# Constants of a two-layer hybrid decoder made in pieces, and attention's two masks turned into one mask and a difference of values

## The chip, the core and the metric

The kernel runs on one core of a Trainium2 chip. The core's engines are TensorE (PE, matmuls; PEld is its weight load), VectorE (DVE), ScalarE (ACT), GpSimd (POOL) and SyncE (SP, which only issues DMAs here); each takes its instructions in order, and they wait for one another by semaphores. The metric is the device time of one execution in microseconds, median of several runs.

## What is computed

Two decoder layers on 1024 tokens of width 1024, then a final norm. Per layer, from the reference (cut):

```python
h = rms_norm(x, norm_w[layer])
proj = h @ w_in[layer]
(q, k, v, z_attn, q_h, f_h, i_h, g_h, gate_attn, gate_hgrn) = jnp.split(proj, split_points, axis=-1)
q, k = partial_rope(q, positions), partial_rope(k, positions)      # 8 heads, 2 KV heads of 64
a = sliding_window_attention(q, k, v, attn_sinks[layer]) * silu(z_attn)   # window 128
logf = log(lb + (1 - lb) * sigmoid(f_h)); kin = (1 - lb) * sigmoid(-f_h); qin = silu(q_h)
o = hgrn2_recurrence(qin, kin, i_h, logf)                          # 4 heads of 128
b = rms_norm_per_head(o) * hgrn_norm_w[layer] * silu(g_h)
merged = sigmoid(gate_attn) * (a @ w_up_attn) + sigmoid(gate_hgrn) * (b @ w_up_hgrn)
x = x + merged @ w_out[layer]
```

`lb` comes from a softmax over the layers, the rotary angles from `positions`, and a query sees its own position and the 127 before it. In blocks of 128 a query of block b therefore sees of block b its own keys up to itself, and of block b-1 the keys behind its own index: each of the 128 index pairs belongs to exactly one of the two.

## The kernel before

Matmuls work on fp32 numbers split in a high and a low part (`whi`, `wlo` of the weights, L128 and L129; three matmuls for each product). A layer runs through these stages: norm and transposes; 13 *pairs* of 128-column chunks of the input projection; rotary, and the projection for `z`; attention, in whose gaps stand the value projection `pi` of the recurrence (L762) and the forget and query projections of its head 0 (L769); the recurrence of the four heads (`core`, L835), with other projections between; the up and out projections.

**A pair** (`pair_rest`, L271) computes two chunks for 1024 tokens by five products of half size, 12 matmuls of 128x512 each. Its weights are two loaded chunks `wr`; DVE adds their halves to `ws` (L277 to L281), ACT casts sums and halves to the high parts (`whi`, L128; `wh`, L285), DVE makes the low parts (`wlo`, L129; `wl`, L286). The products go to two PSUM banks, `pb` and `pc`, and DVE adds them to three outputs `pq` (L303), which ACT puts through sigmoid or silu and sends off (`gate_out`, L473 and L474). Buffers: two for each kind of full weight chunk (`wp`), one for `wh` and `wl`, four for outputs (`hp`, tag `po`).

**Constants.** In the first layer, `constants()` (L356 to L429) is called after pair 1 and `tables()` (L431 to L450) after pair 5. The first loads masks and small inputs, makes `lb` and `oml`, the angles `ang` (eight multiplications, L407), their reduction to one period (`nrn`, L410 to L421), and two Sin on ACT (L426, L427), each change of function family costing an ACT_TABLE_LOAD. The second makes four tables `tab` on POOL and DVE, which PE transposes (`tt`, L447) and ACT sends to memory, where `rotary` reads them in pair 12.

**Attention** goes in steps u: `turn(u-4)` transposes the probabilities of a block (`tp`, L721), `value(u)` projects, then come `values(u-4)`, `scores(u-1)`, `softmax(u-2)`. The probabilities of the window stand in one 128x128 matrix a head: each entry is that of the past block or of the own one. DVE multiplies the transposes by the mask of the past and by the mask of the own block (`side`, two masks) into two halves of `pT` (L724), and `values` (L728) multiplies the first with `vn` of block b-1, the second with `vn` of block b into one bank `av`; ACT copies that to `avo` (L738).

The order of instructions on each engine is made by a scheduler when the program is built, from the order of the code, buffers and its own costs; only operations under `tc.keep_in_program_order` stay as written. PE's order thus follows from the order on other engines, and the reverse.

Of the kernel before, what the change touches and what calls it, by code (L numbers as in the profile page):

```python
# [17 lines left out]
P = 128  # L18
# [20 lines left out]
def trunk_kernel(ctx, tc, x, positions, norm_w, w_in, attn_sinks, hgrn_norm_w, w_up_attn,  # L39
# [315 lines left out]

    def constants():  # L356
# [3 lines left out]
        side = cp.tile([P, 2, P], F32, name="side")  # L360
# [18 lines left out]
        nc.sync.dma_start(lbl, lb_logits.rearrange("l (h p) -> p l h", p=P))  # L379

# [20 lines left out]


# [3 lines left out]
        for b in range(NB):  # L406
            V.tensor_scalar(out=ang[:, b], in0=freq, scalar1=posf[:, b:b + 1], scalar2=None, op0=ALU.mult)  # L407
        nrn = cp.tile([P, NB, HALF], F32, name="nrn")
# [5 lines left out]
        for bits in (2, 8, 8, 24):  # L414
            if bits == 24:
                c = float(np.float32(rest))
            else:
                e = math.floor(math.log2(rest))
                q = 2.0 ** (e - (7 if bits == 8 else 7))
                c = math.floor(rest / q) * q  # L420
            V.scalar_tensor_tensor(out=ang, in0=nrn, scalar=-c, in1=ang, op0=ALU.mult, op1=ALU.add)  # L421
            rest -= c
        V.tensor_scalar(out=ang, in0=ang, scalar1=3.1415925, scalar2=-3.1415925, op0=ALU.min, op1=ALU.max)
# [5 lines left out]
        return ones, side, upper, never, mdiag, mlev, sink, hnw, lb, oml, sins, nrn  # L429

    def tables(sins, nrn):  # L431
        for i in range(2):
            for g in range(2):
                b = slice(4 * g, 4 * g + 4)
# [21 lines left out]
    def first_chunk(L, m, slots):  # L456

        nm = f"p{L}_{m}"
        return (split_slot if slots else split_w)(load_chunk(w_in[L], pairs[m][0][0], nm), nm, [P, KT, P])


    for L in range(DEPTH):
# [135 lines left out]
        for m in range(NPAIR):  # L598
            (c0, r0), (c1, r1) = pairs[m]
            o = pair_rest(wi, (c0, c1), parts, hT, f"{L}_{m}", p1s[m])  # L600
            if m > 9:
                tr[r1] = slot([P, T], f"tr_{L}_{r1}")
            for key, r, t0 in (("22", r1, 512), ("12", r0, 512), ("21", r1, 0)):
                if m < 10:
                    gate_out(o[key], o[key], r, t0)
                else:
                    S.activation(tr[r][:, t0:t0 + 512], o[key], AF.Copy, scale=qkv[r][1])
            if m == 12:
                cosT, sinT = rotary()
            if L == 0 and m == 1:  # L610
                ones, side, upper, never, mdiag, mlev, sink, hnw, lb, oml, *angles = constants()
            elif L == 0 and m == 5:
                tables(*angles)
# [35 lines left out]

        w = [chunk(wi, OZ + j * P, f"z{L}_{j}") for j in range(2)]  # L650
# [16 lines left out]
        z(3, w[3], [H0, H1])  # L667

# [45 lines left out]
        def turn(b):  # L714
            pr, _ = probs[b]
            probs[b] = []
            for g in range(2):

                tp = bank([P, 2, 2, P], f"tp_{L}_{b}_{g}")
                for j in range(4):  # L720
                    PE.transpose(tp[:, j % 2, j // 2], pr[:, 4 * g + j], ident)  # L721
                pT = slot([P, 2, 4, P], f"pT_{L}_{b}_{g}")
                for pt in ([0, 1] if b else [1]):
                    V.tensor_tensor(out=pT[:, pt], in0=tp.rearrange("p r i q -> p (r i) q"),  # L724
                                    in1=side[:, pt].unsqueeze(1).broadcast_to([P, 4, P]), op=ALU.mult)
                probs[b].append(pT)

        def values(b):  # L728
            av = bank([P, 4, P], f"av_{L}_{b}")
            for g, pT in enumerate(probs.pop(b)):  # L730
                for pt in ([0, 1] if b else [1]):
                    for r in range(2):
                        PE.matmul(av[r * HD:(r + 1) * HD, 2 * g:2 * g + 2].rearrange("p h q -> p (h q)"),  # L733
                                  lhsT=vn[0][:, b if pt else b - 1, g * HD:(g + 1) * HD],
# [438 lines left out]
def _constants():  # L1173
    p = np.arange(P)
    past = p[:, None] > p[None, :]
    side = np.stack([past, ~past], axis=1).astype(np.float32)
# [36 lines left out]
```

## Time and profile before

| | |
|---|---|
| three runs, us | 1463.02, 1467.82, 1465.97; median 1465.97 |
| the profiled execution, us | 1462.61 |
| its span, us | 1460.8 |
| busy in the span | PE 97%, PEld 78%, DVE 64%, ACT 46%, POOL 5% |
| time PE waited longest for, by line | `lv_n` on DVE's `gs`: 5.9 us in 6 waits |

A span is the time from the first to the last instruction of one profiled execution. In the rows below, "a <- b" after an operation reads output and input; what stands in square brackets is how long its engine was idle before it, and which instruction on which engine released it. `x4` is the number of such instructions in a row. Matmuls are pipelined: the time of one in a row is the distance between two starts, not the length that the row gives. Names leave buffer numbers out, so `pb`, `wlo_s` and the like recur in every pair.

### The profile page before, as it was taken

Reading aid. Unit: us, or ns where it says so; the run is one execution under the profiler, and the core shown is the slowest. Engines: PE = TensorE matmul, PEld = TensorE weight load, DVE = VectorE, ACT = ScalarE, POOL = GpSimd, SP = SyncE. Lnnn points to the kernel's source line nnn. Section 1 sums busy time; section 2 is a strip of 40 time slices with the busy share of each in tenths; the row PEclk is TensorE's granted clock in tenths of the full one; section 3 lists DMA queues with packets and bytes.
Section 4 is the critical chain, followed back from the end, with each engine's and each line's share of the span. In section 5 each row is a group of like instructions: output and inputs, shape, how many; then the busy total and the mean of one; then the engine's idle time right before and its main releaser. Section 6 shows DMA issues by size and latency. Waiting matters only on the chain.

```text
span 1460.8 us, 21289 instructions
## 1 busy us (share of the span) xinstructions
PE 1420.7 (97%) x8252; PEld 1146.4 (78%) x8252; DVE 933.4 (64%) x1586; ACT 676.4 (46%) x1354; POOL 66.7 (5%) x77
## 2 busy tenths in 40 slices
PE   8999999999999999999999999999999999999998
PEld 7877778878777778778888878887787677787876
DVE  6856656646656887673656466565467588867643
ACT  8754333246664554432556332333567545433321
POOL 1100000310000000000000000003000000000000
PEclk9999999999999999999999999999999999999999
DMA  8433443463236643336454333436522465444431
GB/s 271 158 109 116 141 145 113 155 166 129 81 114 204 222 175 131 120 113 231 158 199 151 102 130 125 149 94 200 164 73 94 138 203 195 140 148 152 159 144 58
DMA packets 194277, 214.41 MB, mean 147 GB/s; under 512 B 12480, under 2 KB 142016, under 8 KB 194176
## 3 DMA queue, kind: packets, MB, share of 16 engines
q1 hardware_dynamic: 161152, 161.66, 34.8%
q10 hardware_dynamic: 31488, 46.15, 8.6%
q0 software_dynamic: 1536, 5.24, 0.9%
q8 instruction: 65, 1.06, 0.3%
q14 instruction: 36, 0.29, 0.1%
HBM read 145.65 MB, written 59.77 MB: 141 GB/s over the span
## 4 chain that ended last, share of the span: by engine, by line
PE 75%; DVE 9%; DMA 7%; ACT 6%; issue 2%; ACTq 0%; SPq 0%; DVEq 0%; POOL 0%
PE pb L291 4%; PE pb L292 4%; PE pb L293 4%; PE pg L263 3%; PE pg L265 3%; PE pg L264 3%; PE pc L291 3%; DMA wr<-in_w_in_dram 2%; PE pc L292 2%; PE pc L293 2%; PE pj_qh L139 2%; PE av L733 2%; PE pj_qh L140 2%; PE pj_qh L141 2%; PE pi L140 2%
## 5 line engine op out<-in xcount | busy, mean ns | idle before, releaser
L128 ACT CAST whi_s<-ws 128x1024 fp32r<-128x1024 f32 x26 | 27.4, 1053 | 129.2 <-DVE ws L278 125.0
L724 DVE TENSOR_TENSOR pT<-tp,side 128x512 f32<-128x512 f32 x60 | 39.2, 681 | 23.5 <-PE tp L721 23.5
L139 PE MATMUL pu_ua<-wh_a,wlo_ua 128*128 128x512 f32 x128 | 51.7, 404 | 0.0
L141 PE MATMUL pu_ua<-wh_a,whi_ua 128*128 128x512 f32 x128 | 50.7, 396 | 0.0
L1160 PE MATMUL po<-wlo_o,mg 128*128 128x512 f32 x128 | 49.9, 390 | 0.8 <-DVE wlo_o L129 0.8
L140 PE MATMUL pu_ua<-wl_a,whi_ua 128*128 128x512 f32 x128 | 50.3, 393 | 0.0
L709 ACT ACTIVATE pr<-pr,mx 128x128 f32<-128x128 f32 x128 | 49.9, 395 | 0.8 <-ACT it L759 0.8
L473 ACT ACTIVATE pq<-pq 128x512 f32<-128x512 f32 x60 | 37.8, 631 | 26.6 <-DVE pq L303 25.2
L1159 PE MATMUL po<-whi_o,mg 128*128 128x512 f32 x128 | 50.0, 391 | 0.1
L263 PE MATMUL pg<-hh,wlo_p 128*128 128x512 f32 (+1 forms) x128 | 47.0, 372 | 3.1 <-POOL wlo_p L129 1.7
L1161 PE MATMUL po<-whi_o,mg 128*128 128x512 f32 x128 | 49.6, 389 | 0.0
L694 DVE COPY_PREDICATED pr<-upper,sc 128x256 f32<-128x256 int32 x56 | 23.2, 443 | 40.4 <-ACT pr L693 40.4
L1082 ACT CAST mg<-u 128x512 fp32r<-128x512 f32 x32 | 19.6, 621 | 61.2 <-DVE u L1080 61.1
L264 PE MATMUL pg<-hl,whi_p 128*128 128x512 f32 (+1 forms) x128 | 46.1, 363 | 0.0
L265 PE MATMUL pg<-hh,whi_p 128*128 128x512 f32 (+1 forms) x128 | 46.0, 363 | 0.0
L277 DVE TENSOR_TENSOR ws<-wr 128x512 f32<-128x512 f32 x26 | 17.9, 690 | 42.2 <-DMA wr<-in_w_in_dram 42.2
L303 DVE TENSOR_TENSOR pq<-pb,p 128x512 f32<-128x512 f32 x40 | 27.6, 690 | 26.6 <-PE pb L293 26.6
L129 DVE TENSOR_TENSOR wlo_t<-ws,whi_t 128x1024 fp32r<-128x1024 f32 x26 | 31.8, 1225 | 18.0 <-ACT whi_t L128 17.9
L263 PE MATMUL pg<-hh,wl_p 128*128 128x512 f32 (+1 forms) x112 | 41.3, 369 | 1.7 <-DVE wl_p L337 1.1
L291 PE MATMUL pb<-th,wlo_s 128*128 128x512 f32 x104 | 40.9, 393 | 2.0 <-DVE wlo_s L129 2.0
L291 PE MATMUL pc<-hh,wlo_t 128*128 128x512 f32 x104 | 41.6, 400 | 0.7 <-DVE pq L303 0.6
L291 PE MATMUL pb<-th,wl 128*128 128x512 f32 x104 | 41.1, 395 | 0.8 <-DVE pq L303 0.7
(394 smaller groups left out, 4452.7 us busy)
## 6 DMA issues: line engine op xcount, KB each, us to landing
wr<-in_w_in_dram SPq DMA_DIRECT2D x64, 512.0 KB
gd<-pq ACTq DMA_DIRECT2D x76, 256.0 KB
wr_p<-in_w_in_dram SPq DMA_DIRECT2D x26, 512.0 KB
fq<-fq ACTq DMA_DIRECT2D x48, 256.0 KB
x<-in_x_dram SPq DMA_DIRECT2D x16, 512.0 KB
ga<-gd SPq DMA_DIRECT2D x16, 512.0 KB
u<-gd SPq DMA_DIRECT2D x16, 512.0 KB
wr_o<-in_w_out_dram SPq DMA_DIRECT2D x16, 512.0 KB
```

The source lines that it names most:

```text
L139: PE.matmul(acc, lhsT=ll, rhs=rh, start=i == 0, stop=False)
L140: PE.matmul(acc, lhsT=lh, rhs=rl, start=False, stop=False)
L141: PE.matmul(acc, lhsT=lh, rhs=rh, start=False, stop=i == n - 1)
L263: PE.matmul(acc, lhsT=wl[:, k], rhs=h[:, t], start=k == 0, stop=False, skip_group_check=q > 0)
L264: PE.matmul(acc, lhsT=wh[:, k], rhs=l[:, t], start=False, stop=False, skip_group_check=q > 0)
L265: PE.matmul(acc, lhsT=wh[:, k], rhs=h[:, t], start=False, stop=k % 4 == 3, skip_group_check=q > 0)
L291: PE.matmul(acc, lhsT=wl[:, k], rhs=h, start=start and k == 0, stop=False, skip_group_check=not start)
L292: PE.matmul(acc, lhsT=wh[:, k], rhs=l, start=False, stop=False, skip_group_check=not start)
L293: PE.matmul(acc, lhsT=wh[:, k], rhs=h, start=False, stop=k == 3, skip_group_check=not start)
L709: S.activation(pr[:, h], pr[:, h], AF.Exp, bias=mx[:, h:h + 1], accum_out=sm[:, h:h + 1])
L1159: PE.matmul(accs[j], lhsT=ll, rhs=wh[:, i], start=k + i == 0, stop=False)
L1160: PE.matmul(accs[j], lhsT=lh, rhs=wl[:, i], start=False, stop=False)
```

## The change

**The constants.** `constants()` becomes a generator with eight yields, and `next(consts, None)` runs its next piece after each pair: after pair 0 the loads and masks, after pair 1 `lb` and `oml`, after pair 2 the positions and `ang`, after pair 3 the reduction, after pair 4 the limits, both Sin and a square, after pairs 5 to 8 one table each. What is computed stays the same; names are handed on by a dictionary `made`.

**Attention.** `side` is one mask, that of the own block. A new tile `vd` holds, for blocks 1 to 7, the values of a block minus those of the block before. `turn` copies the transposes whole into the first half of `pT` on ACT and multiplies them by the one mask into the second half on DVE. `values` multiplies the whole with `vn` of block b-1 and the masked part with `vd`. The number of matmuls is the same.

```diff
--- before.py
+++ after.py
@@ constants @@
     def constants():
...
-        side = cp.tile([P, 2, P], F32, name="side")
+        side = cp.tile([P, P], F32, name="side")
...
+        made.update(ones=ones, side=side, upper=upper, never=never, mdiag=mdiag, mlev=mlev, sink=sink, hnw=hnw)
+        yield
...
         V.tensor_scalar(out=oml, in0=lb, scalar1=-1.0, scalar2=1.0, op0=ALU.mult, op1=ALU.add)
+        made.update(lb=lb, oml=oml)
+        yield
...
             V.tensor_scalar(out=ang[:, b], in0=freq, scalar1=posf[:, b:b + 1], scalar2=None, op0=ALU.mult)
+        yield
...
             V.scalar_tensor_tensor(out=ang, in0=nrn, scalar=-c, in1=ang, op0=ALU.mult, op1=ALU.add)
             rest -= c
+        yield
         V.tensor_scalar(out=ang, in0=ang, scalar1=3.1415925, scalar2=-3.1415925, op0=ALU.min, op1=ALU.max)
...
         S.activation(sins, ang, AF.Sin)
         S.activation(nrn, ang, AF.Sin, scale=0.5)
         V.tensor_tensor(out=nrn, in0=nrn, in1=nrn, op=ALU.mult)
-        return ones, side, upper, never, mdiag, mlev, sink, hnw, lb, oml, sins, nrn
-    def tables(sins, nrn):
         for i in range(2):
             for g in range(2):
+                yield
                 b = slice(4 * g, 4 * g + 4)
                 t = hp.tile([P, 4, P], F32, tag="po", name=f"tab_{i}_{g}")
...
@@ the loop over pairs @@
-            if L == 0 and m == 1:
-                ones, side, upper, never, mdiag, mlev, sink, hnw, lb, oml, *angles = constants()
-            elif L == 0 and m == 5:
-                tables(*angles)
+            next(consts, None)
...
@@ behind the z projection @@
+        vd = slot([P, NB - 1, P], f"vd_{L}")
+        V.tensor_tensor(out=vd, in0=vn[0][:, 1:], in1=vn[0][:, :NB - 1], op=ALU.subtract)
...
@@ turn @@
                 pT = slot([P, 2, 4, P], f"pT_{L}_{b}_{g}")
-                for pt in ([0, 1] if b else [1]):
-                    V.tensor_tensor(out=pT[:, pt], in0=tp.rearrange("p r i q -> p (r i) q"),
-                                    in1=side[:, pt].unsqueeze(1).broadcast_to([P, 4, P]), op=ALU.mult)
+                whole = tp.rearrange("p r i q -> p (r i) q")
+                if b:
+                    S.copy(pT[:, 0], whole)
+                V.tensor_tensor(out=pT[:, 1], in0=whole, in1=side.unsqueeze(1).broadcast_to([P, 4, P]), op=ALU.mult)
                 probs[b].append(pT)
...
@@ values @@
-                                  lhsT=vn[0][:, b if pt else b - 1, g * HD:(g + 1) * HD],
+                                  lhsT=(vd if b and pt else vn[0])[:, b - 1 if b else 0, g * HD:(g + 1) * HD],
...
@@ the mask on the host @@
-    past = p[:, None] > p[None, :]
-    side = np.stack([past, ~past], axis=1).astype(np.float32)
+    side = (p[:, None] <= p[None, :]).astype(np.float32)
```

Where the change moves instructions, three places. The first is pair 3 of the first layer, on two engines, DVE first; `ws_3`, `wlo_3` and `wl_3` are the weights of pair 3, `pq_2` and `pq_3` outputs. Before:

```order
L277 TENSOR_TENSOR ws_3_0_1410<-wr_3_1_1408 128x512
L407 TENSOR_SCALAR ang<-freq,posf 128x8 x8
L303 TENSOR_TENSOR pq_2_22_1331<-pc_2_1334,p_0_2_351 128x512
L410 TENSOR_SCALAR nrn<-ang 128x64
L278 TENSOR_TENSOR ws_3_0_1410<-ws_3_0_1410,wr_3_0_1406 128x512
L411 TENSOR_SCALAR nrn<-nrn 128x64
L280 TENSOR_TENSOR ws_3_1_1411<-wr_3_0_1406,wr_3_1_1408 128x512
```

After:

```order
L303 TENSOR_TENSOR pq_2_21_1308<-pb_2_1309,p_0_2_351 128x512
L412 CAST posf<-posi 128x8
L415 TENSOR_SCALAR ang<-freq,posf 128x8 x8
L129 TENSOR_TENSOR wlo_3_t<-ws_3_1_1398,whi_3_t 128x1024
L286 TENSOR_TENSOR wl_3_1412<-wr_3_1_1395,wh_3_1411 128x512
L303 TENSOR_TENSOR pq_3_12_1415<-pb_3_1418,p_0_2_351 128x512
L419 TENSOR_SCALAR nrn<-ang 128x64
```

`ang` and the reduction no longer stand between the sums `ws_3`; `ang` stands ahead of `wlo_3_t` and `wl_3`, the reduction behind them.

The same place on ACT; `wh_3` is the cast on which `wl_3` waits. Before:

```order
L128 CAST whi_3_t<-ws_3_1_1411 128x1024
L474 DMA gd_138<-pq_2_22_1331 128x512
L426 ACT_TABLE_LOAD
L426 ACTIVATE sins<-ang 128x64
L427 ACTIVATE nrn<-ang 128x64
L473 ACT_TABLE_LOAD
L473 ACTIVATE pq_2_12_1330<-pq_2_12_1330 128x512
L473 ACTIVATE pq_2_21_1332<-pq_2_21_1332 128x512
L474 DMA gd_138<-pq_2_12_1330 128x512
L474 DMA gd_138<-pq_2_21_1332 128x512
L285 CAST wh_3_1424<-wr_3_1_1408 128x512
```

After:

```order
L128 CAST whi_3_t<-ws_3_1_1398 128x1024
L483 ACTIVATE pq_2_21_1308<-pq_2_21_1308 128x512
L285 CAST wh_3_1411<-wr_3_1_1395 128x512
L484 DMA gd_138<-pq_2_21_1308 128x512
L436 ACT_TABLE_LOAD
L436 ACTIVATE sins<-ang 128x64
L437 ACTIVATE nrn<-ang 128x64
L483 ACT_TABLE_LOAD
L483 ACTIVATE pq_3_22_1416<-pq_3_22_1416 128x512
L128 CAST whi_4_s<-ws_4_0_1503 128x1024
```

Sin and its two table loads went from ahead of `wh_3` to behind it, ahead of pair 3's first activation and of `whi_4_s`.

The second place is PE in attention: `av_2` are the value products of block 2, `sc_5` the scores of block 5, `pi_7` a value projection. Before:

```order
L140 MATMUL pi_7_3414<-wlo_i_0_2819,hhi_0_2452 128x512
L733 MATMUL av_2_3337<-pT_2_0_3298,vn_2548 64x256 x2
L685 MATMUL sc_5_0_0_3351<-ks_0_0_2491,qs_1_0_2507 128x256
L685 MATMUL sc_5_0_1_3352<-ks_0_1_2492,qs_1_1_2508 128x256
L733 MATMUL av_2_3337<-pT_2_0_3298,vn_2548 64x256 x2
L689 MATMUL sc_5_0_0_3351<-ks_0_1_2492,qs_1_0_2507 128x256
L733 MATMUL av_2_3337<-pT_2_1_3306,vn_2548 64x256 x2
L689 MATMUL sc_5_0_1_3352<-ks_0_0_2491,qs_1_1_2508 128x256
L685 MATMUL sc_5_0_0_3351<-ks_0_0_2491,qs_2_0_2593 128x256
L733 MATMUL av_2_3337<-pT_2_1_3306,vn_2548 64x256 x2
```

After:

```order
L141 MATMUL pi_6_3311<-wh_i_6_2838,hh_1_3_146 128x512
L746 MATMUL av_2_3339<-pT_2_0_3300,vn_2548 64x256 x2
L746 MATMUL av_2_3339<-pT_2_0_3300,vd_2816 64x256 x2
L746 MATMUL av_2_3339<-pT_2_1_3308,vn_2548 64x256 x2
L746 MATMUL av_2_3339<-pT_2_1_3308,vd_2816 64x256 x2
L697 MATMUL sc_5_0_0_3353<-ks_0_0_2491,qs_1_0_2507 128x256
```

The four pieces between the scores became one block ahead of them.

The third place is ACT at the end of attention, where `fq_0_2_512` is the second half of head 0's query, which the recurrence loads first. Before:

```order
L626 ACT_TABLE_LOAD
L626 ACTIVATE fq_0_2_0_3737<-pj_qh_0_0_0_3712 128x512
L738 COPY avo_6_3749<-av_6_3740 128x512
L629 DMA fq_0_2_2462<-fq_0_2_0_3737 128x512
L739 DMA ad_2474<-avo_6_3749 512x1x128
L626 ACTIVATE fq_0_2_512_3793<-pj_qh_0_1_0_3768 128x512
```

After:

```order
L633 ACTIVATE fq_0_2_0_3739<-pj_qh_0_0_0_3714 128x512
L737 COPY pT_7_0_3759<-tp_7_0_3754 128x512
L636 DMA fq_0_2_2462<-fq_0_2_0_3739 128x512
L751 COPY avo_6_3751<-av_6_3742 128x512
L737 COPY pT_7_1_3767<-tp_7_1_3762 128x512
L752 DMA ad_2474<-avo_6_3751 512x1x128
L633 ACTIVATE fq_0_2_512_3795<-pj_qh_0_1_0_3770 128x512
```

Two copies of `pT_7` went ahead of that activation. On PE the transposes `tp_7` (before: near the end of the query's second half) and `av_6` (before: ahead of it) now stand behind the query, in the second forget projection. Elsewhere on PE, in both layers: `av_7` stands in three pieces instead of four, `av_6` in two instead of one; in the first layer the four sets of `tt` stand one each in pairs 6 to 9, after six matmuls, and `tv_0` is moved from pair 6 to the `z` stage. DMAs are issued in the same order as before.

## Rows read from the trace of the kernel before

**Rows 1.** Page: busy us (share of the span) and instructions by engine.

```profile
PE 1420.7 (97%) x8252; PEld 1146.4 (78%) x8252; DVE 933.4 (64%) x1586; ACT 676.4 (46%) x1354; POOL 66.7 (5%) x77
```

**Rows 2.** Windows: start:end, length, busy PE, PEld, DVE, ACT, POOL, clock, DMA.

```profile
124.50:138.97 14.47, 13.89 (x62) 11.18 (x60) 11.61 (x41) 7.12 (x9) 0.00 (x0) 1.00 0.23 75
138.97:154.70 15.73, 13.76 (x62) 11.08 (x60) 9.22 (x14) 7.86 (x12) 0.00 (x0) 1.00 0.48 155
182.31:200.85 18.54, 16.61 (x82) 13.07 (x80) 10.46 (x28) 6.76 (x10) 1.58 (x3) 1.00 0.48 156
200.85:214.53 13.68, 13.68 (x62) 11.19 (x60) 8.88 (x12) 4.53 (x6) 0.00 (x0) 1.00 0.43 137
214.53:228.29 13.76, 13.76 (x62) 11.19 (x60) 8.64 (x12) 5.69 (x7) 0.00 (x0) 1.00 0.41 132
228.29:242.38 14.09, 13.93 (x61) 11.19 (x60) 8.56 (x13) 4.53 (x6) 0.00 (x0) 1.00 0.41 131
846.11:860.26 14.15, 13.94 (x61) 11.19 (x60) 8.61 (x13) 4.53 (x6) 0.00 (x0) 1.00 0.40 130
860.26:874.23 13.97, 13.90 (x62) 11.19 (x60) 9.15 (x13) 4.53 (x6) 0.00 (x0) 1.00 0.42 134
```

**Rows 3.** Timeline of PE: start, length, line, operation [idle before <-releaser].

```profile
154.70 0.50 PE L291 MATMUL pb<-th,wlo_s 128*128 128x512 f32 x1 [1.97 <-DVE wlo_s L129]
...
183.70 0.63 PE L447 MATMUL tt<-ident,tab 128*128 128x128 f32 x4
...
184.40 0.39 PE L292 MATMUL pb<-tl,whi_s 128*128 128x512 f32 x1
...
190.73 0.63 PE L447 MATMUL tt<-ident,tab 128*128 128x128 f32 x4 [1.07 <-DVE tab L440]
```

**Rows 4.** Timeline of DVE, pairs 2 and 3.

```profile
131.59 1.16 DVE L407 TENSOR_SCALAR ang<-freq,posf 128x8 f32<-128x8 f32 x8
...
145.22 0.69 DVE L286 TENSOR_TENSOR wl<-wr,wh 128x512 fp32r<-128x512 f32 x1
...
149.69 0.69 DVE L277 TENSOR_TENSOR ws<-wr 128x512 f32<-128x512 f32 x1 [1.67 <-DMA wr<-in_w_in_dram]
```

**Rows 5.** Timeline of ACT, pair 3.

```profile
138.62 1.28 ACT L426 ACT_TABLE_LOAD   x1
...
143.24 0.62 ACT L285 CAST wh<-wr 128x512 fp32r<-128x512 f32 x1 [0.45 <-ACT pq L473]
```

**Rows 6.** Window in the middle of attention, columns as in rows 2.

```profile
400.00:440.00 40.00, 40.00 (x225) 29.27 (x225) 21.51 (x44) 26.93 (x73) 1.84 (x2) 1.00 0.38 125
```

**Rows 7.** Instructions on `pT`: count, ns min/median/max, first and last start.

```profile
L724 DVE TENSOR_TENSOR pT<-tp,side x60: 639/682/693, 360.9 to 1150.4; 128x512 f32<-128x512 f32 x60
```

**Rows 8.** Timeline, DVE before attention and ACT in it.

```profile
335.85 1.23 DVE L129 TENSOR_TENSOR wlo_i<-wr_i,whi_i 128x1024 fp32r<-128x1024 f32 x1 [1.68 <-ACT whi_i L128]
...
375.16 0.59 ACT L759 COPY it<-pi 128x512 f32<-128x512 f32 x1 [3.91 <-PE pi L141]
```

**Rows 9.** Timeline of PE, value products between others.

```profile
375.05 1.95 PE L733 MATMUL av<-pT,vn 128*64 128x256 f32 x16
...
376.93 0.50 PE L685 MATMUL sc<-ks,qs 128*128 128x256 f32 x2
...
386.88 0.65 PE L733 MATMUL av<-pT,vn 128*64 128x256 f32 x4
...
387.78 0.65 PE L733 MATMUL av<-pT,vn 128*64 128x256 f32 x4
```

**Rows 10.** Timeline of ACT, DVE and PE, end of attention.

```profile
434.86 0.60 ACT L626 ACTIVATE fq<-pj_qh 128x512 f32<-128x512 f32 x1 [5.96 <-PE pj_qh L141]
...
444.17 1.22 DVE L883 TENSOR_TENSOR gs<-R,Q 128x1024 f32<-128x1024 f32 x1 [6.52 <-DMA Q<-fq]
...
446.78 0.64 PE L890 MATMUL lv_n<-gs,ones 128*32 128x256 f32 x8
```

**Rows 11.** Waits of PE, whole span: us in total, times, longest.

```profile
PE lv_n L890 <- DVE gs L883: 5.9, 6, 1.8
```

More of the change, by code (lines that the diff above doesn't have):

```diff
@@ L354, in trunk_kernel @@
     tabs = [dp.tile([P, T], F32, name=f"tabs_{i}") for i in range(2)]
+    made = {}
     def constants():
@@ L459, in first_chunk @@
         return (split_slot if slots else split_w)(load_chunk(w_in[L], pairs[m][0][0], nm), nm, [P, KT, P])
+    consts = constants()
     for L in range(DEPTH):
@@ L648, in z @@
             colsA(w[0], w[1], hT, f"z{L}_{j}", use, groups)
+        ones, side, upper, never, mdiag, mlev, sink, hnw, lb, oml = (
+            made[n] for n in "ones side upper never mdiag mlev sink hnw lb oml".split())
         w = [chunk(wi, OZ + j * P, f"z{L}_{j}") for j in range(2)]
```

## The prediction, made before the changed kernel was run

> **What bounds the kernel now.** I read the page's busy times first. PE is busy 1420.7 of the 1460.8 us span [rows 1], so all idle time of PE together is some 40 us, and nothing that shortens DVE, ACT or a queue can bring more than that. The change can move time in two ways only: by taking idle time out of PE, or by changing the order on PE where that order itself costs something. The span was part of an execution of 1462.61 us; the median of the three runs is 1465.97, 3.36 more. My sum is made in the trace and carried to the median by adding it to 1465.97.
>
> Next I cut the first layer's projection pairs out of the trace, one window each from the first matmul of a pair to that of the next [rows 2]. A pair has 60 matmuls and takes 13.76 us when nothing disturbs it, 0.23 us a matmul. Pair 3 takes 15.73 us and pair 6 takes 18.54. In the second layer, where no constants are made, pairs 2 and 3 take 14.15 and 13.97. That is what the constants cost now, and where.
>
> Then the waits of PE in the two long pairs [rows 3]: 1.97 us before pair 4's first matmul, on the low part of its weights' sum (`wlo_s`); 1.07 us before the fourth table's transposes (`tt`). The tables' transposes themselves are PE work: from the start of one set of four to the second matmul behind it is 0.70 us, of which one matmul is 0.23, so a set costs 0.47.
>
> Where does the 1.97 come from? On DVE [rows 4] pair 3's `wl` starts at 145.22, 6.25 us into the pair, and pair 4's `ws` begins only at 149.69, when its weights land; the buffers of the weights are few and the next load starts when the readers of the old one are done. `wl` waited for `wh`, and on ACT [rows 5] `wh` is at 143.24, behind the Sin's table load at 138.62, the two Sins, the load back and two gate activations: 4.62 us in one run. So the stall is a chain: Sin on ACT, `wh`, `wl`, load, `ws`, `wlo_s`, PE.
>
> For attention I looked at a stretch in its middle [rows 6]: PE is busy 40.00 of 40 us, DVE 21.51, ACT 26.93. PE waits for nothing there. That decides what the new masks are worth.
>
> **Part A, the constants in pieces.** What is computed is the same, only placed otherwise.
>
> Pair 2: 14.47 us now, with the constants' small DVE operations between the `ws` additions; the same pair without them 14.15 [rows 2]. They leave it. −0.3.
>
> Pair 3: in the new order Sin and its two table loads stand behind `wh`, so the chain above loses 4.62 us at its head. But the eight multiplications `ang` (1.16 us, [rows 4]) now stand ahead of `wlo_3_t` and `wl_3`, and the two loads stand ahead of the gate activations of pair 3 itself. The target is 13.97, the same pair of the second layer; I keep 0.25 for the 1.16 us that is now in front of `wl`. 15.73 becomes 14.2: −1.5. Bounds: −1.76 if nothing is left, −0.3 if the chain is merely replaced (below).
>
> Tables: pairs 6 to 9 take 18.54 + 13.68 + 13.76 + 14.09 = 60.07 [rows 2]. With one set of transposes in each they cost at best 4 × (13.76 + 0.47) = 56.92, that is −3.15. The transposes of the values (`tv`), which stood in pair 6, go to a later stage with their own cost of one set, +0.47. That is −2.68. One table in pair 6 waited 1.07 us because DVE made it late; spread out, each set has a whole pair's time of DVE (8.6 to 10.5 us busy of some 14, by the windows), yet DVE runs in order and the set's place on PE is fixed after six matmuls; I keep a third of one such wait, 0.35. −2.35. Bounds: −2.68 and, with 0.4 us of waiting for every set, −1.1.
>
> Part A: −0.3 − 1.5 − 2.35 = −4.15, between −4.75 and −1.7.
>
> **Part B, the masks.** Each layer loses 14 DVE multiplications (`pT` by the past's mask), 0.68 us each [rows 7], and gains 14 ACT copies of the same shape out of PSUM, 0.59 us each by the nearest row, the eviction of a value projection [rows 8]. That is 9.5 us off DVE and 8.3 us onto ACT. On PE it is worth nothing in itself: the matmul count is equal, PE is full in that stretch, and ACT has 13.07 us idle in 40 [rows 6], DVE 18.49. I take 0; the cost if ACT's cover were gone is rival 3. The difference `vd` is one DVE subtraction a layer, 128x896 where 128x1024 takes 1.23 us [rows 8], so about 1.09 us (estimate, by length); it stands just before `wlo_i_2`, in a place where DVE has gaps of 1.68 us [rows 8]. I take 0, and 1.09 a layer as the upper end. Every block now also waits for `vd`, but it is made well before the first block.
>
> The order on PE does change. In the old order the value products of block 2 (`av_2`) came in four pieces between score products; in the new one they stand in one block. A block of 16 records takes 1.88 us (375.05 to 376.93) and its two switches some 0.1 each, 2.07 in all; one piece of four with one score matmul of half a usual matmul's length takes 0.90 (386.88 to 387.78), so 0.78 a piece and 3.12 for four [rows 9]. −1.05. `av_7` goes from four pieces to three, the first of them beside its neighbour: −0.3. `av_6` goes from one block to two pieces: +0.25. Some −1.1 a layer, −2.2 in all. Bounds: 0 if the scheduler's order makes other switches that I overlooked as dear, −2.6.
>
> The end of attention is moved against this. The second half of head 0's query is activated on ACT directly behind its last matmul now (434.86); the recurrence loads it, DVE makes `gs` from it at 444.17 to 445.39, and PE wants `gs` at 446.78 [rows 10], with 1.4 us to spare. In the new order ACT has `pT_7_0`, `avo_6` and `pT_7_1` ahead of that activation, and PE has the transposes `tp_7_0`, `tp_7_1` and most of `av_6` ahead of those. Counting what stands on PE from the query's last matmul to the end of `tp_7_1`: seven matmuls of 0.23 (1.6), pieces of `av_6` (2.2), two sets of transposes (0.5 each), 4.8 us; with the copy of 0.59 the activation comes 5.4 us behind the query instead of at once. PE itself reaches `gs` later too: 46 matmuls (10.5) + `av_6` 2.2 + `av_7` 2.6 + transposes 1.0 = 16.3 us behind the query, where it was 11.95. So data at 10.57 + 5.4 = 15.97 against demand at 16.3: the slack falls from 1.4 to 0.3. A miss of a microsecond either way is likely in such a count; the waits for `gs` of the other heads went up to 1.8 us a time [rows 11]. I take 0.4 a layer, +0.8; bounds 0 and 1.6 a layer.
>
> Part B: −2.2 + 0.8 = −1.4, bounds −2.6 and +3.2.
>
> **Sum:** −4.15 − 1.4 = −5.55; 1465.97 − 5.55 = 1460.4, call it **1460.5**.
>
> **Rival 1: the recurrence starts late.** The slack of 0.3 is wrong by two microseconds and PE stands 1.6 us or more before `gs` in each layer. For it: four operations newly ahead of one activation. Against it: PE has also got more work before it needs the result. −4.15 − 2.2 + 3.2 = −3.15, some 1462.5: within the resolution.
>
> **Rival 2: the constants' stalls move instead of going away.** The two table loads and the Sins (the 4.62 us, less the two gate activations) now stand before pair 3's own gate activations and pair 4's `whi_4_s`; if they make that cast late, PE waits for `wlo_4_s` all the same, and each table's transposes wait a little in their own pair. Pair 3 then gives 0.3, the tables 1.1, pair 2 0.3: −1.7 − 1.4 = −3.1, some 1462.9. Against it: the casts now stand behind gate work that is not urgent.
>
> **Rival 3, slower: ACT becomes the pace of attention.** DVE's multiplication waits for ACT's copy of the same transposes, and DVE works in order: when ACT is late, all that stands behind the multiplication is late, the maxima of the next scores too, then the exponentials on ACT itself. It decides when ACT's free time per block, 13.07/40 of some 10.3 us or 3.4 us [rows 6], no longer holds the two copies, 1.18 us, in the places where they are wanted. If all 28 reached PE: 28 × 0.59 = 16.5, less 6.35 of gains, +10.2: some 1476. The order built puts the copy first and makes the multiplication wait; in the trace of before only DVE reads those transposes, so no row shows the pair. The Trainium skill, page "PSUM — Partial Sum Buffer", section "PSUM bank collisions raise a hardware error", says that two engines must not touch the same bank and quadrant at once, ScalarE and VectorE reading included, and that software has to order them; by it copy and multiplication can never overlap, 0.59 + 0.68 = 1.27 us for a set against twice 0.68 now, so the transposes gain no latency, and the rival stays open; without the rule the two could run side by side and it would fall.
>
> **How the numbers follow.** Two medians of this kernel can be told apart from about 0.3%, 4.4 us, so faster means below 1461.6. Chances: forecast 0.53, rival 1 0.21, rival 2 0.17, rival 3 0.09. The forecast lies only 1 us beyond that bound, so of its 0.53 I count 0.40 as faster and 0.13 as same; of rivals 1 and 2 (and their milder forms) 0.11 as faster, 0.26 as same, 0.01 slower. Faster 0.51, same 0.39, slower 0.10. Range: the low end takes all of A (−4.75) and of the block order (−2.6) at no late start, −7.35, and 1.6 us for the spread of the runs: 1457. The high end is rivals 1 and 2 together, −1.7 − 2.2 + 3.2 = −0.7, 1465.3, and some spread: 1466. Rival 3 is left out.
>
> **What would show it.** Pairs 3 and 6 at 14.0 to 14.3 us each, the waits before `pb` on `wlo_s` and before `tt` on `tab` gone; one `tt` set in each of pairs 6 to 9. `av_2` in one block. DVE's `pT` waiting for ACT's `pT`, and PE waiting for neither. ACT some 8 us busier in each attention, DVE some 9 us less. Head 0's `gs` some 5 us later, and a wait of PE before it near 0.4. The forecast falls if PE is no longer full in the middle of attention (rival 3), if head 0 waits well over 1 us (rival 1), or if pairs 3 and 6 to 9 keep more than half of their surplus (rival 2).

## The result, and the profile after

The changed kernel takes 1457.56 us in the median of six runs (1455.14 to 1461.16), the kernel before 1465.8 in six runs: a ratio of 0.9944, 95% interval 0.9928 to 0.9961. That is 8.2 us less, faster by more than the 0.3% that can be told apart, and inside the forecast range (1457 to 1466, forecast 1460.5). The profiled execution of the change took 1457.39 us, its span is 1455.6; against [rows 1] the span is 5.2 us shorter. So the traces show 5.2 us, the runs 8.2.

The page of the change, busy time of each engine, to be held against [rows 1]:

```profile
PE 1418.9 (97%) x8252; PEld 1147.8 (79%) x8252; DVE 922.0 (63%) x1560; ACT 690.0 (47%) x1382; POOL 65.5 (5%) x77
```

DVE has 11.4 us less, ACT 13.6 more. Of the 5.2 us of the span PE's idle time is 3.4 and its busy time 1.8, so what DVE and ACT do is not the gain; it lies in PE's waits and in the order of its matmuls.

**The pairs.** Windows of pairs 2, 3 and 6 to 9 in the change, columns as in [rows 2], one pair in each row:

```profile
124.83:139.00 14.17, 13.91 (x61) 11.18 (x60) 9.13 (x23) 7.37 (x9) 0.00 (x0) 1.00 0.45 149
139.00:152.60 13.60, 13.60 (x61) 11.26 (x60) 11.35 (x30) 7.37 (x10) 0.00 (x0) 1.00 0.32 97
...
180.03:195.00 14.97, 14.43 (x65) 11.49 (x64) 8.65 (x16) 5.11 (x7) 0.53 (x1) 1.00 0.45 139
195.00:209.37 14.37, 14.29 (x65) 11.57 (x64) 9.58 (x17) 5.11 (x7) 0.53 (x1) 1.00 0.48 149
209.37:224.31 14.94, 14.48 (x66) 11.50 (x64) 7.93 (x15) 5.37 (x8) 0.53 (x1) 1.00 0.42 125
224.31:238.45 14.14, 14.14 (x66) 11.58 (x64) 9.35 (x17) 5.93 (x8) 0.00 (x0) 1.00 0.41 141
```

Pair 3 has no idle time left (13.60 of 13.60) although DVE does 11.35 us of work in it, two more than before. In the kernel before pair 10 is such a pair:

```profile
242.38:255.98 13.60, 13.60 (x61) 11.27 (x60) 8.22 (x13) 3.89 (x5) 0.23 (x1) 1.00 0.27 88
```

Pairs 6 to 9 take 58.42 together where they took 60.07; pairs 6 and 8 still hold half a microsecond of idle each. There PE waits for an addition `pq`. The first rows are DVE and PE in pair 6, the last two DVE in pair 7:

```profile
190.27 1.23 DVE L129 TENSOR_TENSOR wlo_s<-ws,whi_s 128x1024 fp32r<-128x1024 f32 x1 [0.45 <-ACT whi_s L128]
191.41 0.68 DVE L303 TENSOR_TENSOR pq<-pb,pq 128x512 f32<-128x512 f32 x1
...
192.15 0.50 PE L291 MATMUL pb<-th,wl 128*128 128x512 f32 x1 [0.54 <-DVE pq L303]
...
204.81 0.68 DVE L303 TENSOR_TENSOR pq<-pb,pq 128x512 f32<-128x512 f32 x1
205.41 1.21 DVE L129 TENSOR_TENSOR wlo_s<-ws,whi_s 128x1024 fp32r<-128x1024 f32 x1
```

In pairs 6 and 8 the addition that frees the bank `pb` stands behind the weights' `wlo_s` on DVE, in pair 7 ahead of it. The table's own operations on DVE ended nine to ten microseconds earlier. The weights' sums `ws` begin some 0.4 us later than in a pair without a table (6.57 us into pair 6, 6.14 into pair 7 of the kernel before), but in pair 7 of the change, where they begin as late (6.67), PE waits for no addition.

The whole stretch from pair 0 to pair 10, the first row of the kernel before, the second of the change:

```profile
96.67:242.38 145.71, 140.89 (x621) 113.89 (x621) 92.68 (x164) 55.84 (x73) 2.11 (x4) 1.00 0.41 131
```

```profile
97.04:238.45 141.41, 139.99 (x618) 113.52 (x617) 92.18 (x164) 55.70 (x73) 2.11 (x4) 1.00 0.42 132
```

That is 4.30 us. The moved transposes `tv_0` give 0.46 back in the first layer's `z` stage (46.35 us before, 46.81 after).

**Attention.** From the first value product to the first product `l` of the recurrence, in the first layer, before and after (the second layer reads the same, 100.32 and 99.17):

```profile
365.57:465.90 100.33, 100.33 (x684) 74.95 (x683) 62.32 (x128) 60.62 (x166) 1.95 (x3) 1.00 0.36 118
```

```profile
361.89:461.06 99.17, 99.17 (x683) 75.06 (x682) 54.66 (x114) 67.43 (x180) 1.93 (x3) 1.00 0.36 119
```

PE is busy without a gap in both. DVE does 7.7 us less, ACT 6.8 more, and the stretch is 1.16 shorter. What makes it shorter is the order on PE: the value products of a layer stand in 15 separate pieces before and in 12 after. `av_2` in the change stands, on PE's timeline, in one block of 16 records from 381.74 to 383.62, 1.88 us as in [rows 9]:

```profile
381.74 0.65 PE L746 MATMUL av<-pT,vn 128*64 128x256 f32 x4
...
383.08 0.60 PE L746 MATMUL av<-pT,vd 128*64 128x256 f32 x4
383.62 0.50 PE L697 MATMUL sc<-ks,qs 128*128 128x256 f32 x2
```

The copies and multiplications of `pT` (count, duration min/median/max in ns; then who waited for them, us and times):

```profile
L738 DVE TENSOR_TENSOR pT<-tp,side x32: 678/682/692, 357.2 to 1148.2; 128x512 f32<-128x512 f32 x32
L737 ACT COPY pT<-tp x28: 564/582/589, 367.5 to 1147.5; 128x512 f32<-128x512 f32 x28
...
  DVE pT L738: 10.1, 4
  ACT avo L751: 9.3, 10
```

DVE waits 10.1 us for ACT's copies, in four places, and no matmul is among those that wait (the last row is ACT's `avo`, which waits for the value products). The end of attention, timeline of ACT, DVE and PE, to be held against [rows 10]:

```profile
432.62 0.60 ACT L633 ACTIVATE fq<-pj_qh 128x512 f32<-128x512 f32 x1
...
441.74 1.23 DVE L896 TENSOR_TENSOR gs<-R,Q 128x1024 f32<-128x1024 f32 x1 [6.32 <-DMA Q<-fq]
...
443.54 0.64 PE L903 MATMUL lv_n<-gs,ones 128*32 128x256 f32 x8
```

`gs` ends at 442.97, PE takes it at 443.54 with no wait: of 1.4 us of slack 0.6 is left.

**A place that the change doesn't touch** is longer in this execution. The second layer's `z` stage takes 1.47 us more than before: PE waited 1.9 us for the low part of the reloaded input, and then ran for 3 us at half clock. Windows, the clock is the third column from the right (1.00 is 2.4 GHz, 0.50 is 1.2 GHz):

```profile
1006.00:1009.10 3.10, 1.23 (x6) 0.69 (x4) 1.94 (x2) 2.09 (x2) 0.00 (x0) 1.00 0.88 245
...
1010.00:1013.20 3.20, 3.20 (x9) 2.52 (x8) 2.08 (x2) 2.30 (x3) 0.00 (x0) 0.50 1.12 289
```

The sum in the traces: pairs -4.30, `tv_0` +0.46, attention 2 x -1.16, the `z` stage +1.47, and -0.5 over the rest (before pair 0 +0.4, behind the second layer's attention -1.3, small differences between): -5.2. The traces are one execution each, and that of the kernel before has no stretch at half clock but in its last microseconds.

### The profile page after: what moved, and what is told of

Read it like the earlier page. It is cut to its first block, busy times and chain, and to the rows that moved or that the text cites. A ratio compares the mean times of both kernels' runs of the same rounds, so it can differ in the third digit from the quotient of the medians.

```text
span 1455.6 us, 21289 instructions
## 1 busy us (share of the span) xinstructions
PE 1418.9 (97%) x8252; PEld 1147.8 (79%) x8252; DVE 922.0 (63%) x1560; ACT 690.0 (47%) x1382; POOL 65.5 (5%) x77
## 4 chain that ended last, share of the span: by engine, by line
PE 76%; DMA 8%; DVE 8%; ACT 5%; issue 2%; SPq 0%; ACTq 0%; DVEq 0%
PE pb L291 4%; PE pb L292 4%; PE pb L293 4%; PE pg L263 3%; PE pg L265 3%; PE pg L264 3%; PE pc L291 2%; PE pc L292 2%; PE pc L293 2%; DMA wr<-in_w_in_dram 2%; PE pj_qh L139 2%; PE pj_qh L141 2%; PE pj_qh L140 2%; PE av L746 2%; PE pi L140 2%
## 5 line engine op out<-in xcount | busy, mean ns | idle before, releaser
L813 ACT COPY u<-pu_ua 128x512 f32<-128x512 f32 x32 | 18.8, 588 | 47.3 <-PE pu_ua L141 47.2
```

## The experiments

Ratios are to the kernel before on the same chip; e1 to e11 number the runs. Theory: part A pays by idle time of PE in the first layer's pairs, part B by fewer separate pieces of value products on PE. Rivals: the masks' work pays by itself; all comes from one of the two.

**The two halves.** First part A alone (e1), with `turn`, `values` and `side` as before; against the change:

```diff
-                if b:
-                    S.copy(pT[:, 0], whole)
-                V.tensor_tensor(out=pT[:, 1], in0=whole, in1=side.unsqueeze(1).broadcast_to([P, 4, P]), op=ALU.mult)
+                for pt in ([0, 1] if b else [1]):
+                    V.tensor_tensor(out=pT[:, pt], in0=tp.rearrange("p r i q -> p (r i) q"),
+                                    in1=side[:, pt].unsqueeze(1).broadcast_to([P, 4, P]), op=ALU.mult)
...
```

> Only part A: constants and tables in pieces behind the pairs, attention as in the kernel before. Theory (most of the gain is PE idle time in the first layer's pairs 2, 3 and 6 to 9): the pairs of layer 0 take 4.3 us less in the trace, 0.5 of it comes back with the transposes moved to the z stage; some 3.8 us off the time, ratio 0.997 to 0.998. The value products keep their old pieces, attention its length. Rival (the time comes from attention's masks): within 1 us of the kernel before.

Measured: 0.9965 (0.9948 to 0.9982), 1459.97 against 1465.06 us, 5.1 less. The pairs in its trace:

```profile
97.06:238.21 141.15, 139.77 (x617) 113.61 (x617) 92.04 (x164) 55.69 (x73) 2.11 (x4) 1.00 0.42 132
```

-4.56 where the change has -4.30, and attention keeps its 100.32. Then part B alone (e2), against the change:

```diff
-            next(consts, None)
+            if L == 0 and m == 1:
+                ones, side, upper, never, mdiag, mlev, sink, hnw, lb, oml, *angles = constants()
+            elif L == 0 and m == 5:
+                tables(*angles)
...
```

> Only part B: one mask, the difference of values, the copy on ACT; constants as in the kernel before. Theory (attention gains only by fewer separate pieces of the value products on PE): 1.1 us less in each layer's attention, pairs unchanged (15.7 us for pair 3, 18.5 for pair 6): -2.2 us, ratio 0.998 to 0.999. Rival (less work on DVE pays by itself): the same sign but more, 3 us or more, and shorter stretches elsewhere in attention. Rival (ACT becomes the pace): slower by up to 10 us.

Measured: 0.9979 (0.9966 to 0.9993), 2.6 less; pair 3 is 15.67 and pair 6 18.65, as before, attention 99.17. The halves add up: 5.1 + 2.6 = 7.7 against 8.2. By its time alone (interval 1.0 to 5.0 us) part B can't tell the theory's 2.2 from the rival's 3; the next two runs do.

**Masks or order?** Part B alone, with the copy on DVE (e4):

```diff
-                    S.copy(pT[:, 0], whole)
+                    V.tensor_copy(pT[:, 0], whole)
```

> Part B with the whole copy on DVE instead of ACT, constants as in the kernel before: one mask and the difference of values stay, and the value products on PE stand in the same pieces as in the kernel before (four for blocks 2 and 7). Theory (only the order of PE pays): no change, within 0.5 us in the trace. Rival (one mask or the difference of values itself pays): 2 us faster like part B alone. Rival (the subtraction vd costs): 1.1 us slower in each layer, before attention.

Measured: 0.9997 (0.9981 to 1.0013). The first layer's attention, part B alone above and with the copy on DVE below:

```profile
366.15:465.32 99.17, 99.17 (x682) 75.05 (x682) 54.63 (x114) 67.41 (x180) 1.92 (x3) 1.00 0.36 119
```

```profile
366.78:467.10 100.32, 100.32 (x682) 74.93 (x681) 62.31 (x128) 60.60 (x166) 1.92 (x3) 1.00 0.35 118
```

One mask and the difference of values are in both. With the copy on DVE the value products are in the old 15 pieces and the stretch is the old one to 0.01 us; with the copy on ACT they are in 12. So the algebra pays nothing, `vd` costs nothing, and moving work off DVE pays by the order alone that the scheduler then makes. The cross test (e5) leaves the masks as they were and changes the order:

```diff
         def attend(u):
-            if u > 3:
-                values(u - 4)
             if 0 < u <= NB:
                 scores(u - 1)
+            if u > 3:
+                values(u - 4)
```

> The kernel before with one edit: in a step of attention the scores are written ahead of the values, so that every block's value products stand in one piece on PE (before: four pieces for blocks 2 and 7, two for block 5); the two masks on DVE and the constants stay as before. Theory (a separate piece costs 0.35 us by its two switches, whoever makes the masks): seven pieces fewer in a layer, 2.4 us less in each layer's attention, -4.9 us, ratio 0.9965 to 0.998. Rival (the gain of part B comes from moving the copy to ACT or from the difference of values): no change. Rival (values written later start the recurrence later): attention itself shorter, but PE waits for gs in head 0, at most half of the gain left.

Measured: 0.9974 (0.9961 to 0.9987), 3.8 us by the ratio, within what the theory said. The value products stand in 8 pieces. In the second layer the stretch from the first scores to the recurrence takes 133.90 us, before 136.11: -2.2, near the 2.4 of seven pieces. In the first it is only 0.4 shorter, since at its start PE waited 1.3 us for a cast, where before it was 0.3, and then ran at half clock. Of the third expectation, a wait for `gs` in head 0, 0.4 us came in the first layer and nothing in the second. The wait for the cast:

```profile
PE pi L139 <- ACT whi_i L128: 1.3, 1, 1.3
```

Order without the masks gains about as much as the masks do (3.8 against 3.1 us by the ratios, and the intervals overlap). Both together, the same edit on the changed kernel (e6):

> The changed kernel with the same edit, scores ahead of values: blocks 2 and 7 in one piece, blocks 5 and 6 in two. Theory: two pieces fewer in a layer than in the changed kernel, 0.7 us a layer, -1.4 us against the change, ratio to the kernel before 0.992 to 0.995. Rival: the wait for gs in head 0 comes up and the time is that of the change or longer.

Measured: 0.9951 (0.9936 to 0.9965), 1457.38 us: no different from the change. There are 10 pieces. The second layer's stretch from the first scores is 1.2 us shorter than the change's (134.16 against 135.35), but in the first the same cast made PE wait 1.5 us, and two stretches at half clock, in its `z` and attention stages, cost 1.7 us each. It does not beat the change.

**Part A taken apart.** First without its last step, the four tables together (e3; the edit against part A alone):

```diff
             for g in range(2):
-                yield
+                if i == 0 and g == 0:
+                    yield
```

> Part A without its last step: the pieces up to the two Sin as in the change, but the four tables together behind pair 5 as in the kernel before; attention as before. Theory (two separate gains): pairs 2 and 3 short (14.2 and 13.6 us), pair 6 long as before (18.5 us): -2.5 us, 1.2 to 1.7 us slower than the pieces alone. Rival (one cause for all, late constants): pairs 6 to 9 get shorter as well and the time is that of the pieces alone.

Measured: 0.9974 (0.9963 to 0.9985), 1461.19 us, 1.2 above part A alone. Pairs 2 and 3 take 14.29 and 13.60 as expected; pair 6 takes 20.27, longer than the 18.54 of before. After its two waits (the window's first row) PE ran at half clock (the second):

```profile
186.50:190.50 4.00, 2.04 (x12) 1.34 (x11) 3.83 (x11) 1.53 (x2) 0.52 (x1) 0.99 0.21 79
190.50:193.90 3.40, 3.40 (x10) 2.64 (x9) 1.09 (x1) 0.00 (x0) 0.00 (x0) 0.51 0.73 229
```

3.40 us at 0.51 lose 1.7; without them the pair takes 18.6, the length of before. The reverse, the tables one by one and the other constants together as before (e8):

```diff
...
             elif L == 0 and m == 5:
-                tables(*angles)
+                made = tables(*angles)
+                next(made)
+            if L == 0 and m > 4:
+                next(made, None)
```

> The kernel before with one edit: the tables one each behind pairs 5 to 8 instead of all four behind pair 5; the other constants together behind pair 1 as before. Theory (two gains that don't depend on each other): pair 3 stays at 15.7 us, pairs 6 to 9 together take 58.0 to 58.5 us instead of 60.07. Rival (late angles make the tables late): pairs 6 to 9 stay at 60.

One execution: pair 3 takes 15.67, pairs 6 to 9 together 58.12. The two gains don't depend on each other. And behind pair 4's wait, which this kernel still has, the clock fell, which it had not done in the trace of before:

```profile
153.00:155.10 2.10, 0.19 (x2) 0.11 (x1) 1.85 (x3) 1.70 (x3) 0.00 (x0) 1.00 0.62 188
155.10:158.40 3.30, 3.30 (x9) 2.53 (x10) 1.83 (x2) 0.83 (x2) 0.00 (x0) 0.53 0.61 200
```

Then the chain that the prediction named, with both Sin alone moved (e7, also one execution), against the kernel before:

```diff
...
+    def sines(ang, nrn):
         V.tensor_scalar(out=ang, in0=ang, scalar1=3.1415925, scalar2=-3.1415925, op0=ALU.min, op1=ALU.max)
...
+            elif L == 0 and m == 4:
+                angles = sines(*angles)
             elif L == 0 and m == 5:
                 tables(*angles)
```

> The kernel before with one edit: both Sin, the limits and the square are written behind pair 4 instead of with the other constants behind pair 1; the other constants and the tables stay. On ACT the Sin and its table loads then stand behind wh_3. Theory (the wait of pair 4 is the chain Sin, wh, wl, weight load, ws, wlo_s): pair 3 takes 13.6 to 14.0 us instead of 15.73, pair 2 stays at 14.4. Rival (the eight multiplications and the reduction on DVE between the sums make it): pair 3 stays near 15.7.

Neither: pair 3 takes 14.98, and pairs 4 and 5 take 14.09 and 14.15 where they took 13.73 and 13.88, so that pairs 2 to 5 together gain 0.2. The chain did what it was said to: `wl` is at 140.42 (before 145.22) and the weights land at 146.47 (before 149.69); PE no longer waits for `wlo_s`. But look at DVE:

```profile
140.42 0.68 DVE L286 TENSOR_TENSOR wl<-wr,wh 128x512 fp32r<-128x512 f32 x1
...
146.47 0.69 DVE L277 TENSOR_TENSOR ws<-wr 128x512 f32<-128x512 f32 x1 [3.33 <-DMA wr<-in_w_in_dram]
...
147.69 0.68 DVE L303 TENSOR_TENSOR pq<-pc,p 128x512 f32<-128x512 f32 x1
```

It stood 3.33 us before the weights, and the addition that frees the bank `pc` is queued behind them. PE waited for that instead:

```profile
PE pc L291 <- DVE pq L303: 1.6, 2, 1.1
```

In the change the reduction's small operations stand in that gap and the addition stands ahead of `ws_4`:

```profile
144.75 0.68 DVE L303 TENSOR_TENSOR pq<-pc,p 128x512 f32<-128x512 f32 x1
...
146.91 0.69 DVE L277 TENSOR_TENSOR ws<-wr 128x512 f32<-128x512 f32 x1 [1.11 <-DMA wr<-in_w_in_dram]
```

So moving Sin is not enough: pairs 2 to 5 take 57.81 us before, 57.64 with Sin moved and 55.20 in the change, where the other pieces are moved too. That it is the addition's place that saves the time, and not the operations that fill the gap, is read from the queue; it was not tried apart. Nor was the other half, the other pieces moved and Sin left.

**What the runs gain beyond the traces.** Runs list a mean granted clock: 0.9965 over 70 runs of the kernel before (standard error 0.0002), 0.9977 for part A alone (0.0003, 6 runs), 0.9964 for part B alone (0.0004, 12 runs). Over these 70 a run with 0.001 less clock is 1.1 us longer (0.8, 1.4 and 1.2 in the three groups that ran together; correlation -0.65). In proportion, 0.001 of 1465 us would be 1.5. Theory: the two waits that part A removes are followed by half clock in part of the runs. The test (e11) puts idle time back into the changed kernel:

```diff
+        if nm in ("0_4", "0_11", "1_11"):
+            for _ in range(2):
+                V.tensor_tensor(out=f[0], in0=f[0], in1=f[0], op=ALU.max)
         h0, l0 = split_w(f[0], f"{nm}_s", [P, 2, 4, P])
```

> The changed kernel with idle time put into PE at three places: two extra DVE operations of 128x1024 (2.4 us) that leave their operand as it is, between the weight sums of pair 4 and pair 11 of the first layer and pair 11 of the second and their low parts, which are ready 0.7, 0.3 and 0.3 us before PE wants them. PE then waits some 1.8, 2.1 and 2.1 us, as it did before pair 4 in the kernel before. Theory (an idle gap of this size is followed in part of the runs by some 3.4 us at half the granted clock, which is what the runs gain beyond the trace): 6 us of waits in the trace, but 7.5 to 10 us in the median of the runs against the change, and the mean granted clock falls by 0.001 to 0.003. Rival (idle costs its own length alone): 6 to 6.5 us, mean clock as in the change.

Measured: 1.0021 (1.0008 to 1.0034), against the change's 0.9944 some 11 us, in medians 9.6. The trace's waits are longer together than I expected (1.4, 2.7 and 3.1 us):

```profile
PE pb L294 <- DVE wlo_s L129: 7.2, 3, 3.1
```

One of the three was followed by half clock in the profiled execution, the second row here, behind the wait of 2.7 us in the first row; the wait of 3.1 us was not:

```profile
252.00:256.00 4.00, 1.80 (x11) 1.28 (x9) 4.00 (x6) 2.60 (x5) 0.00 (x0) 1.00 0.02 5
256.00:259.50 3.50, 3.02 (x7) 2.44 (x8) 1.66 (x2) 0.95 (x2) 1.90 (x2) 0.55 0.99 292
```

The mean clock of its 11 runs is 0.9951 (0.0004), against 0.9973 (0.0003) of the next kernel (e9), whose time is the change's, and 0.9972 (0.0009) of the change itself: 0.0022 of 1465 us is 3.2 us. 7.2 and 3.2 make 10.4, within what was measured. The rival, idle time at its own length, falls by the clock; by the times alone, 9.6 to 11 against 7.2 with intervals of some 2 us each, it would be close. One thing stays open: the same trace has two more stretches at half clock, from 311 and 338 us, where the edit did nothing, behind waits of 2.0 and 1.2 us. Which gaps the lower clock of the other ten runs stands behind, no run shows.

**A better version?** Two attempts at the wait in the `z` stage. Changing the order of the reloads (e9):

```diff
-        for i, (part, nm) in enumerate(((hT.hi, "hi"), (hT.lo, "lo"))):
-            for j in range(2):
+        for j in range(2):
+            for i, (part, nm) in enumerate(((hT.hi, "hi"), (hT.lo, "lo"))):
```

> The changed kernel with one edit: behind the pairs, the reloads of the second half of the normed input are issued as high 0, low 0, high 1, low 1 instead of high 0, high 1, low 0, low 1. In the trace of the change PE waits in the z stage for the low part (0.7 us in the first layer, 1.9 in the second, the latter followed by 3.4 us at half the granted clock). Theory: these waits get shorter, 2 to 4 us off the time of the change, ratio to the kernel before 0.990 to 0.994. Rival (the loads wait for something else that comes no earlier): the wait only changes its name, same time as the change, 0.994 to 0.996.

Measured: 0.9952 (0.9936 to 0.9968), the change's time: the rival. The second layer's `z` stage now waits for the weights' low part, as long as before for the input:

```profile
PE pj_z L139 <- DVE wlo_z L129: 1.7, 1, 1.7
```

And the same loads issued ahead of the rotary tables (e10):

```diff
             if m == 12:
+                for i, (part, nm) in enumerate(((hT.hi, "hi"), (hT.lo, "lo"))):
+                    for j in range(2):
+                        part[1][j] = slot([P, 2, 512], f"h{nm}_{L}_{j}", F32R)
+                        nc.sync.dma_start(part[1][j].bitcast(F32), hd[i][j])
                 cosT, sinT = rotary()
...
```

> The changed kernel with one edit: the same reloads are issued ahead of the rotary tables instead of behind them. Theory: the wait for the low part goes, at the price that the rotary loads come later; 1 to 3 us off the time of the change. Rival (the rotary work on the first queries and keys is then what the z stage or the first scores wait for): 1 to 4 us slower than the change.

Measured: 1.0012 (1.0001 to 1.0022), 1465.29 us, 7.7 us above the change's median and 10 by the ratios, more than the rival said. The first scores wait for the queries, 6.3 us in each layer, and half clock follows both, 3.4 us lost each time:

```profile
PE sc L697 <- DMA qs<-ql: 12.5, 2, 6.3
```

## Why the prediction was right, step by step

- **Pair 2:** -0.3 forecast, -0.30 measured (14.47 to 14.17).
- **Pair 3:** -1.5 forecast, -2.13 measured. The target, the second layer's 13.97, and the 0.25 on top were both too careful: the pair has no idle time at all now. A pair that nothing disturbs takes 13.60, as pair 10 of the kernel before does, and not the 13.76 that I read. The mechanism was half told. The chain from Sin to the weights is there, but breaking it alone (e7) gained 0.75 in the pair and gave 0.6 back in the two behind it; the prediction named the queue on ACT and not the one on DVE.
- **Tables:** -2.35 forecast with `tv_0` counted, -1.65 + 0.46 = -1.19 measured. This was the mis-sized term. The transposes wait for their tables no longer (0.24 of loss once), but pairs 6 and 8 lose 0.70 and 0.62 (counted between starts of matmuls) to additions of `pq` that the built order put behind `wlo_s`. The tables make the weights some 0.4 late in all of these pairs, but only where the order is this one does PE wait; the prediction looked for waits on the tables alone. Pair 6 was expected at 14.0 to 14.3 and takes 14.97. I had put 0.35 for it all; the lower bound, -1.1, was the better guess.
- **Part A:** -4.15 forecast; -4.30 + 0.46 = -3.84 in the trace, two errors that cancel; that the sum came out near is luck. In the runs of part A alone 5.1.
- **Masks and `vd`:** 0 forecast, 0 measured (e4). Rival 3, ACT as the pace, didn't occur: DVE did wait 10.1 us for ACT's copies, as the built order said, and PE never. The rule of the Trainium skill that the prediction set beside it (page "PSUM — Partial Sum Buffer", section "PSUM bank collisions raise a hardware error": two engines on one bank and quadrant have to be kept in order) agrees with the trace in so far as the multiplication stands behind the copy of the same bank, with 10.1 us of waiting in four places; what would happen without that order, no run shows.
- **Pieces of value products:** -1.1 a layer forecast, -1.16 measured in both layers, in the trace of the change as in that of part B alone.
- **Head 0's start:** 0.4 a layer forecast, 0 measured. The count from the query's end was good: data at 15.97 forecast and 15.85 measured, demand at 16.3 and 16.42, so that the slack is 0.57 and not 0.3. Rival 1 needed 1.6. (Its own sum, -3.15, gives 1462.8 and not 1462.5.)
- **Rival 2**, moved stalls, occurred in part, in pairs 6 and 8, at 1.3 us in all.
- **Not in the prediction:** the clock. An idle gap was priced at its length. Part A's mean clock is 0.0012 higher, worth some 1.3 to 1.7 us in the median run (an estimate, by the 1.1 us for 0.001 above or in proportion). With it the parts come to -3.84 - 2.32 - 1.3 to 1.7 = -7.5 to -7.9; measured 8.2, within its interval of 5.7 to 10.5. For the change itself the clock has been taken in six runs only (0.9972, standard error 0.0009), so the share rests on part A alone and on the kernel with added idle time, not on the change's own runs.
- **The number:** the change gained 2.7 us more than the 5.55 forecast, and 1457.56 lies near the low end of the range, which was all gains at their upper bounds and 1.6 us for the spread of the runs. That both parts pay, and where, was foreseen; that the total stayed inside is in part luck.

## What to carry to other kernels

Where PE is full, work that is moved from one engine to another pays by the order that it leaves on PE, so look at the built order before the busy times: here the same algebra gained 1.16 us a layer or nothing, by which engine made a copy. When a long operation is moved off an engine's queue, follow every in-order queue past the place: an addition behind a weight load took over the stall that a Sin had made. Price a gap of one to three microseconds in PE at more than its length: 7.2 us in three gaps cost 9.6 to 11 here.

## What the runs showed of the hardware

An idle gap of PE was followed by a stretch at a granted clock of 0.50 to 0.55 (1.2 instead of 2.4 GHz) in some executions and not in others: behind pair 4's wait of 1.97 us the clock stayed at 1.00 in the trace of the kernel before and fell to 0.53 behind 1.91 us in that of e8, which runs the same instructions there. The length of the gap did not decide it: the clock fell behind 1.2 us in e11 (with 0.3 more close by) and stayed up behind 3.1 us in the same trace. A matmul of 128x512 takes 0.43 us instead of 0.23 in such a stretch (e8), and one stretch costs some 1.7 us (one minus the clock, summed over its windows; 1.6 to 1.7 in all that were single). Profiled executions without one before their last microseconds list a mean clock of 0.998 or 0.999 (the kernel before, e7, e9), those with three 0.995 (e6, e11). Over the 70 runs of the kernel before, 0.001 less mean clock goes with 1.1 us more, so a part of the spread between runs of one kernel goes with the number of such stretches.

A piece of value products between other matmuls costs 0.32 to 0.39 us by its two switches (2.2 us for seven in e5, 1.16 for three in the change; the estimate from [rows 9] was 0.35), though PE shows no idle time there.
